# Loading and multiplying the first two blocks of k's weights among q's first blocks

## The chip, the core and the metric

The kernel runs on one core of a Trainium2 chip. The core has five engines with queues of their own: TensorE (PE; its weight loads, PEld, overlap its matmuls), VectorE (DVE), ScalarE (ACT), GpSimd (POOL) and SyncE (SP), which here issues nearly all transfers (DMA) from the chip's memory (HBM) to on-chip memory (SBUF). PE writes to accumulators in eight banks of PSUM. The metric is the device time of one execution in microseconds (us).

## The reference

The reference is one decoder layer over 256 tokens of width 1024. Its start, cut to what matters here:

```
h = rms_norm(x, attn_norm_g)                 # x * rsqrt(mean(x^2) + eps) * g
proj = h @ w_in                              # 1024 x (6 x 512 + 8 + 2048)
qa, ka, va, qb, kb, vb, f_logit, g_logit = split(proj)
qa = partial_rope(rms_norm(qa heads), pos)   # the same for ka
o_a = moba_attention(qa, ka, va)             # causal: 256 tokens are one block
o_b = forgetting_attention(rms_norm(qb), rms_norm(kb), vb, log_sigmoid(f_logit + b))
merged = gate_a * (o_a @ w_moba) + gate_b * (o_b @ w_fox)
x = x + merged @ w_out
x = x + conv_ffn(rms_norm(x))                # 1024 -> 2 x 2816 -> 1024
```

All is float32. The norm's factor per token, rsqrt(mean(x^2)), is a number per row of the product, so it can be applied after the product with w_in; g belongs to the rows of w_in and goes in before.

## The kernel before, in words

**Products of split numbers.** PE multiplies float32 operands in a shortened format (fp32r). To keep precision, each operand is split into a high part and a low part: ACT copies it into the high part (`whi` for weights, `xh` for x), DVE subtracts to get the low part (`wlo`, `xl`). A product is then three: xh·whi, xh·wlo, xl·whi.

**Blocks.** `project(m, pt, h)` forms one of six products of x with 512 columns (m = 0 is q, 1 is k, 2 is v of the first branch, 3 to 5 those of the second). The 1024 inputs are eight k-blocks of 128; h chooses four of them. For each k-block there are three pairs of matmuls of 512 columns (the two of a pair, t = 0 and 1, are the two halves of the tokens and write to two banks). Before the change q's eight blocks are multiplied first, then k's first four, then the matmul for the norm (`norm1`, L227), the products of the forget gate (L318), then k's other four, v's, and so on.

**The lead.** q's weights and x itself come in eight transfers `lead[k]`, each 384 KB: 256 values of x and 512 weights for each of 128 rows. `lead(p)` issues two of them and records the splitting of two blocks: `split_x(k)` makes `xh` and `xl` with the norm's weights g (for k = 0 the high part is made on DVE, L160, later on ACT, L162; the low part on DVE, L163), L102 makes `whi` on ACT, L103 `wlo` on DVE. g comes in a transfer of its own (4 KB), issued by ACT.

**The other weights.** `load` brings every further chunk of 1 MB into one of three buffers `raw` (SP issues; L131) and splits it in halves of 1024 columns (L134 on ACT, L135 on DVE) into one of six pairs of buffers `whi`/`wlo`. k's first chunk alone is fetched as two transfers of 512 KB. A raw buffer is free when both halves are split, a `whi`/`wlo` pair when PE has used it. At most eight transfers of SP stand open: each waits for the one eight before it.

**The norm.** Behind the split of k's first chunk ACT squares x (L181, two instructions), DVE adds the squares up (L183 to L186, with a `wlo` of L135 between), PE sums over partitions (L227), and DVE and ACT turn that into the factor `rs` (L202 to L207, with ACT's L203 and L204). DVE copies the forget gate's products (L320) between. Then `finish_qk` normalizes the heads of q and k and rotates them (up to L279), and `turn_qk` transposes them on PE (L295): first q's, sixteen loads and matmuls, then k's sixteen.

**The order.** On PE the instructions stand in the order in which the code issues them. On ACT, DVE and SP a scheduler sets the order when the program is built; on the chip each engine then works strictly in that order.

**The start.** DVE clears a tile of 512 bf16 numbers, with which PE does eight matmuls whose result nobody reads (L170, the warm-up); then the first block begins.

The table names the lines around the change, before and after (the same code under two numbers):

| step | before | after |
|---|---|---|
| transfers of the lead | L95 | L101, L102, L104 |
| transfers of k's first two blocks | in L131 | L107 |
| whi, wlo of the lead (ACT, DVE) | L102, L103 | L117, L120 |
| whi, wlo of k's first two blocks | in L134, L135 | L124, L125 |
| xh for k = 0 (DVE), xh (ACT), xl (DVE) | L160, L162, L163 | L184, L186, L190 |
| warm-up matmuls | L170 | L197 |
| whi, wlo of other weights | L134, L135 | L160, L161 |
| matmuls of `project` | L249 | L272 |

Of the kernel before, what the change touches and what calls it, by code (L numbers as in the profile page):

```python
# [8 lines left out]
F32 = mybir.dt.float32  # L9
# [8 lines left out]
P = 128  # L18
# [12 lines left out]
RB, HB, AHEAD = 3, 6, 5  # L31
NWARM = 8
GAPS = (160, 192)
# [8 lines left out]
def decoder_block(ctx, tc, a, out):  # L42
# [7 lines left out]
    def T(shape, tag, bufs=1, dt=F32):  # L50
        return sb.tile(shape, dt, tag=tag, bufs=bufs, name=tag)
# [21 lines left out]

    lt = T([P, KT, LW], "lead")
    xT = lt[:, :, 0:S]
# [16 lines left out]
    def lead(p):  # L92

        for k in (2 * p, 2 * p + 1):
            nc.sync.dma_start(lt[:, k], a["lead"][k])  # L95
        hi = T([P, 1024], "whi", HB, F32R)
        lo = T([P, 1024], "wlo", HB, F32R)
        for j in range(2):
            w = lt[:, 2 * p + j, S:]
            s = slice(j * W4, (j + 1) * W4)  # L100
            split_x(2 * p + j)  # L101
            whi = nc.scalar.activation(hi[:, s], w, AF.Copy)  # L102
            nc.vector.tensor_tensor(lo[:, s], w, hi[:, s].bitcast(F32), op=ALU.subtract)  # L103
        split[("qkv", 0, p // 2), p % 2] = (hi, lo, whi)  # L104

    def home(n):
# [9 lines left out]
    def load(upto):  # L116
        while state["next"] <= min(upto, 2 * len(chunks) - 1):  # L117
            i, h = divmod(state["next"], 2)
            state["next"] += 1
            if i < 2:  # L120
                lead(2 * i + h)
                continue
            c = chunks[i]
            if h == 0:  # L124
                w = 1024 if i == 2 else 2048  # L125
                src = a[c[0]]
                for j in (c[1] - (c[0] == "qkv"), *c[2:]):
                    src = src[j]
                raw = state["raw"] = T([P, 2048], "raw", RB)
                for j in range(2048 // w):  # L130
                    nc.sync.dma_start(raw[:, j * w:(j + 1) * w], src[:, j * w:(j + 1) * w])  # L131
            raw = state["raw"][:, h * 1024:(h + 1) * 1024]
# [14 lines left out]
    sm = T([P, C_END], "sm")  # L147
    g1 = T([P, KT], "g1")
    nc.scalar.dma_start(g1, a["g1"])

# [6 lines left out]
    def split_x(k):  # L157
        g, x = g1[:, k:k + 1], xT[:, k]
        if k == 0:
            nc.vector.tensor_scalar_mul(xh[:, k], x, g)  # L160
        else:  # L161
            nc.scalar.activation(xh[:, k], x, AF.Copy, scale=g)  # L162
        nc.vector.scalar_tensor_tensor(xl[:, k], x, g, xh[:, k].bitcast(F32), op0=ALU.mult, op1=ALU.subtract)  # L163


    warm = T([P, 512], "sq", 2, BF16)
    nc.vector.memset(warm, 0.0)
    wp = bank()
    for j in range(NWARM):
        nc.tensor.matmul(wp, warm[:, 0:P], warm, start=True, stop=True)  # L170

# [67 lines left out]
    V = T([P, NT, 2 * W4], "V")  # L239

    def project(m, pt, h):
        for hh in range(2):
            wh, wl = use(("qkv", m, h), hh)
            for k2 in range(2):
                k = 4 * h + 2 * hh + k2
                rh, rl = (pairs(w[:, k2 * 512:(k2 + 1) * 512]) for w in (wh, wl))
                for i, (lhs, rhs) in enumerate(((xh, rh), (xh, rl), (xl, rh))):
                    for t in range(NT):
                        nc.tensor.matmul(pt[t], lhs[:, k, t * P:(t + 1) * P], rhs, start=(k == 0 and i == 0), stop=(k == KT - 1 and i == 2))  # L249

# [489 lines left out]
def _layout(i):  # L740
# [9 lines left out]
    lead = np.concatenate([x.T.reshape(KT, P, S), w6[:, :W4].reshape(KT, P, W4)], 2)  # L750
    a["lead"] = c(lead)
    a["wf"] = c(k128(w[:, 6 * W4:6 * W4 + NH]))
# [11 lines left out]
    sm = np.empty((P, C_END), f)  # L764
    a["g1"] = c(i["attn_norm_g"][0].reshape(KT, P).T)
    sm[:, C_G2:C_G2 + 8] = i["ffn_norm_g"][0].reshape(KT, P).T
# [41 lines left out]
```

## Time and profile before

| | |
|---|---|
| time, median of 3 runs | 353.95 us (353.94 to 354.75) |
| the profiled execution | 353.87 us, of which the span of its instructions 352.1 us |
| PE busy | 346.8 us, 99% |
| DVE busy | 282.8 us, 80% |
| ACT busy | 225.2 us, 64% |
| from HBM | 67.65 MB, 195 GB/s over the span |

In the lines of the profile, L12 is line 12 of the kernel. A row of the timeline gives the start in us, the time to the end of the last of its instructions, the engine, line and operation, the tiles (written<-read), the shape, how many instructions were merged (x2), and in brackets how long the engine had idled before and what ended that. A row for a stretch gives its bounds and length in us, then the busy time of PE, PEld, DVE, ACT and POOL with the number of instructions in brackets, the clock recorded for PE as a share, the share in which the 16 transfer engines were busy, and GB/s. In the page's list of queues stand packets, megabytes and the share of the 16 engines' time. PE's matmuls overlap, so the start of one to the start of the next tells its pace, not its length.

### The profile page before, as it was taken

Reading aid. Unit: us, or ns where it says so; the run is one execution under the profiler, and the core shown is the slowest. Engines: PE = TensorE matmul, PEld = TensorE weight load, DVE = VectorE, ACT = ScalarE, POOL = GpSimd, SP = SyncE. Lnnn points to the kernel's source line nnn. Section 1 sums busy time; section 2 is a strip of 40 time slices with the busy share of each in tenths; the row PEclk is TensorE's granted clock in tenths of the full one; section 3 lists DMA queues with packets and bytes.
Section 4 is the critical chain, followed back from the end, with each engine's and each line's share of the span. In section 5 each row is a group of like instructions: output and inputs, shape, how many; then the busy total and the mean of one; then the engine's idle time right before and its main releaser. Section 6 shows DMA issues by size and latency. Waiting matters only on the chain.

```text
span 352.1 us, 5895 instructions
## 1 busy us (share of the span) xinstructions
PE 346.8 (99%) x2282; PEld 312.2 (89%) x2282; DVE 282.8 (80%) x533; ACT 225.2 (64%) x404; POOL 1.3 (0%) x8
## 2 busy tenths in 40 slices
PE   8999999999999999999999999999999999999995
PEld 4888888899989989998899989989898989989885
DVE  4899979995796568994489999897879788797633
ACT  5977575858698566662497975765665666565320
POOL 0000000000000000000000000000000000000000
PEclk9999999999999999999999999999999999999999
DMA  7988865566333607865119556674565456550003
GB/s 267 407 340 302 302 236 167 201 232 238 123 122 108 248 6 253 336 247 169 72 45 374 196 224 239 217 262 151 208 239 171 192 235 203 173 223 2 0 0 121
DMA packets 13597, 69.09 MB, mean 196 GB/s; under 512 B 1529, under 2 KB 4737, under 8 KB 6145
## 3 DMA queue, kind: packets, MB, share of 16 engines
q1 hardware_dynamic: 12368, 67.65, 52.8%
q10 hardware_dynamic: 1200, 1.06, 0.9%
q8 instruction: 18, 0.29, 0.3%
q14 instruction: 11, 0.08, 0.1%
HBM read 67.65 MB, written 1.06 MB: 195 GB/s over the span
## 4 chain that ended last, share of the span: by engine, by line
PE 97%; DMA 1%; ACT 0%; SPq 0%; DVE 0%; issue 0%
PE bank L654 22%; PE bank L249 17%; PE bank L700 16%; PE bank L655 11%; PE bank L581 6%; PE bank L454 4%; PE bank L455 4%; PE bank L456 4%; PE bank L551 2%; PE bank L553 2%; PE bank L552 2%; PE bank L387 2%; PE bank L428 2%; DMA lead<-in_lead 1%; PE bank L414 1%; PE bank L295 1%
## 5 line engine op out<-in xcount | busy, mean ns | idle before, releaser
L135 DVE TENSOR_TENSOR wlo<-raw,whi 128x1024 fp32r<-128x1024 f32 x91 | 110.6, 1223 | 24.1 <-ACT whi L134 23.6
L134 ACT ACTIVATE whi<-raw 128x1024 fp32r<-128x1024 f32 x91 | 94.9, 1053 | 39.1 <-PE bank L654 12.8
L654 PE MATMUL bank<-pp,whi 128*128 128x512 f32 x240 | 79.3, 382 | 0.0
L655 PE MATMUL bank<-pp,wlo 128*128 128x256 f32 x240 | 65.4, 273 | 0.0
L654 PEld LDWEIGHTS bank<-pp,whi 128*128 128x128 f32 x240 | 45.4, 189 | 6.3
L655 PEld LDWEIGHTS bank<-pp,wlo 128*128 128x128 f32 x240 | 46.1, 192 | 0.2
L454 PE MATMUL bank<-xh,whi 128*128 128x256 f32 x128 | 35.4, 277 | 0.0
L455 PE MATMUL bank<-xl,whi 128*128 128x256 f32 x128 | 35.2, 275 | 0.0
L456 PE MATMUL bank<-xh,wlo 128*128 128x256 f32 x128 | 35.2, 275 | 0.0
L249 PE MATMUL bank<-whi,xh 128*128 128x512 f32 x96 | 29.0, 384 | 0.3 <-DVE xh L160 0.2
L249 PE MATMUL bank<-wlo,xh 128*128 128x512 f32 x96 | 28.8, 382 | 0.0
L249 PE MATMUL bank<-whi,xl 128*128 128x512 f32 x96 | 28.6, 379 | 0.0
L454 PEld LDWEIGHTS bank<-xh,whi 128*128 128x128 f32 x128 | 24.6, 192 | 0.3 <-DVE nm L392 0.2
L455 PEld LDWEIGHTS bank<-xl,whi 128*128 128x128 f32 x128 | 24.6, 192 | 0.0
L456 PEld LDWEIGHTS bank<-xh,wlo 128*128 128x128 f32 x128 | 24.6, 192 | 0.0
L700 PE MATMUL bank<-whi,qT 128*128 128x512 f32 x72 | 22.4, 379 | 0.0
L670 DVE TENSOR_TENSOR sq<-bank,lows 128x256 f32<-128x256 f32 x44 | 18.2, 418 | 4.9 <-ACT lows L669 4.9
L249 PEld LDWEIGHTS bank<-whi,xh 128*128 128x128 f32 x96 | 17.7, 189 | 4.3 <-ACT whi L102 1.2
L249 PEld LDWEIGHTS bank<-wlo,xh 128*128 128x128 f32 x96 | 17.9, 189 | 3.4 <-DVE wlo L103 1.0
L669 ACT ACTIVATE lows<-bank 128x256 f32<-128x256 f32 x44 | 15.8, 367 | 7.5 <-PE bank L655 7.5
L249 PEld LDWEIGHTS bank<-whi,xl 128*128 128x128 f32 x96 | 18.1, 189 | 2.6
L654 PE MATMUL bank<-pp,bias 128*128 128x512 f32 x56 | 18.9, 385 | 0.0
(196 smaller groups left out, 704.6 us busy)
## 6 DMA issues: line engine op xcount, KB each, us to landing
raw<-in_wu SPq DMA_DIRECT2D x22, 1024.0 KB, 4.8
raw<-in_wd SPq DMA_DIRECT2D x11, 1024.0 KB, 4.8
raw<-in_qkv SPq DMA_DIRECT2D x9, 1024.0 KB, 7.1
raw<-in_wg SPq DMA_DIRECT2D x8, 1024.0 KB, 4.9
raw<-in_wb SPq DMA_DIRECT2D x4, 1024.0 KB, 4.8
raw<-in_wo SPq DMA_DIRECT2D x4, 1024.0 KB, 5.4
lead<-in_lead SPq DMA_DIRECT2D x8, 384.0 KB, 5.9
raw<-in_qkv SPq DMA_DIRECT2D x2, 512.0 KB, 7.7
```

What stands on the lines that cost most here:

```text
L134: whi = nc.scalar.activation(hi, raw, AF.Copy)
L135: wlo = nc.vector.tensor_tensor(lo, raw, hi.bitcast(F32), op=ALU.subtract)
L249: nc.tensor.matmul(pt[t], lhs[:, k, t * P:(t + 1) * P], rhs, start=(k == 0 and i == 0), stop=(k == KT - 1 and i == 2))
L454: nc.tensor.matmul(o, wh[:, w], rh, start=(k == 0 and i == 0), stop=False)
L455: nc.tensor.matmul(o, wh[:, w], rl, start=False, stop=False)
L456: nc.tensor.matmul(o, wl[:, w], rh, start=False, stop=(k == KT - 1 and i == 1))
L581: nc.tensor.matmul(acc[t][dh], lhs[:, k, t * P:(t + 1) * P], rhs, start=(k == 0 and i == 0), stop=(k == KT - 1 and i == 2))
L654: nc.tensor.matmul(two[i], wh[:, w], both, start=(k == 0), stop=False)
L655: nc.tensor.matmul(two[i][:, 0:S], wl[:, w], high, start=False, stop=(k == KT - 1))
L669: nc.scalar.activation(lows[:, i:i + 1].rearrange("p b (a t) -> p b a t", a=2), apart(two[i][:, S:2 * S], 1), AF.Copy)
L670: nc.vector.tensor_tensor(halves(ev[:, i:i + 1]), apart(two[i][:, 0:S], 1), halves(lows[:, i:i + 1]), op=ALU.add)
L700: nc.tensor.matmul(o, lhs, rhs, start=(first and i == 0), stop=(end and i == 2))
```

## The change

It does five things, all at the start of the program. (1) The first lead block comes as two transfers: its weights (256 KB), and then x with the norm's weights g in front (132 KB); g's own transfer is gone, and g1 is now the first eight columns of the tile `lead`. (2) The first two k-blocks of k's weights, which were the first 512 KB of k's first chunk, come as two transfers of 256 KB, one behind the first lead block and one behind the second, and are split there, into one more pair of `whi`/`wlo`; the chunk's second half is fetched later as before. (3) PE multiplies each of these two blocks right behind the q block with the same k, and k's loop leaves them out later. (4) For the first block the low part of the weights is made ahead of the low part of x. (5) There are seven warm-up matmuls instead of eight, on a tile of 128 numbers that is read four times over.

```diff
-NWARM = 8
+NWARM = 7
...
-    lt = T([P, KT, LW], "lead")
+    lead_all = T([P, KT + KT * LW], "lead")
+    g1 = lead_all[:, 0:KT]
+    lt = lead_all[:, KT:].rearrange("p (k w) -> p k w", k=KT)
...
     def lead(p):
+        if p == 0:
+            raw = state["raw"] = T([P, 2048], "raw", RB)
+            k_hi, k_lo = T([P, 1024], "whi", HB, F32R), T([P, 1024], "wlo", HB, F32R)
         for k in (2 * p, 2 * p + 1):
-            nc.sync.dma_start(lt[:, k], a["lead"][k])
+            if k == 0:
+                nc.sync.dma_start(lt[:, 0, S:], a["lead_w"])
+                nc.sync.dma_start(lead_all[:, 0:KT + S], a["lead_x"])
+            else:
+                nc.sync.dma_start(lt[:, k], a["lead"][k - 1])
+            if p == 0:
+                s = slice(k * W4, (k + 1) * W4)
+                nc.sync.dma_start(raw[:, s], a["qkv"][0][0][:, s])
         hi = T([P, 1024], "whi", HB, F32R)
         lo = T([P, 1024], "wlo", HB, F32R)
         for j in range(2):
-            w = lt[:, 2 * p + j, S:]
+            k = 2 * p + j
+            w = lt[:, k, S:]
             s = slice(j * W4, (j + 1) * W4)
-            split_x(2 * p + j)
+            if k:
+                split_x(k)
+                split_low(k)
             whi = nc.scalar.activation(hi[:, s], w, AF.Copy)
-            nc.vector.tensor_tensor(lo[:, s], w, hi[:, s].bitcast(F32), op=ALU.subtract)
+            if k == 0:
+                split_x(k)
+            wlo = nc.vector.tensor_tensor(lo[:, s], w, hi[:, s].bitcast(F32), op=ALU.subtract)
+            if k == 0:
+                after(split_low(k), wlo)
+            if p == 0:
+                k_whi = nc.scalar.activation(k_hi[:, s], raw[:, s], AF.Copy)
+                nc.vector.tensor_tensor(k_lo[:, s], raw[:, s], k_hi[:, s].bitcast(F32), op=ALU.subtract)
         split[("qkv", 0, p // 2), p % 2] = (hi, lo, whi)
+        if p == 0:
+            split[("qkv", 1, 0), 0] = (k_hi, k_lo, k_whi)
...
+            if (i, h) == (2, 0):
+                continue
             c = chunks[i]
-            if h == 0:
-                w = 1024 if i == 2 else 2048
+            if i == 2:
+                nc.sync.dma_start(state["raw"][:, 1024:], a["qkv"][0][0][:, 1024:])
+            elif h == 0:
...
-    warm = T([P, 512], "sq", 2, BF16)
+    warm = T([P, 128], "sq", 2, BF16)
...
-        nc.tensor.matmul(wp, warm[:, 0:P], warm, start=True, stop=True)
+        nc.tensor.matmul(wp, warm, warm[:, None, :].to_broadcast([P, 4, P]), start=True, stop=True)
...
+    def block(pt, w2, k):
+        rh, rl = (pairs(w[:, k % 2 * 512:(k % 2 + 1) * 512]) for w in w2)
+        for i, (lhs, rhs) in enumerate(((xh, rh), (xh, rl), (xl, rh))):
+            for t in range(NT):
+                nc.tensor.matmul(pt[t], lhs[:, k, t * P:(t + 1) * P], rhs, start=(k == 0 and i == 0), stop=(k == KT - 1 and i == 2))
+
     def project(m, pt, h):
         for hh in range(2):
...
+            if (m, h, hh) == (1, 0, 0):
+                continue
+            w2 = use(("qkv", m, h), hh)
+            if (m, h, hh) == (0, 0, 0):
+                wk = split.pop((("qkv", 1, 0), 0))[:2]
+            for k in (4 * h + 2 * hh, 4 * h + 2 * hh + 1):
+                block(pt, w2, k)
+                if m == 0 and k < 2:
+                    block(pk, wk, k)
```

What that does to SP's queue, at the start of the program (`lead` is the tile of x, q's weights and now g; `raw` holds k's weights), before:

```order
L95 DMA lead<-in_lead 128x768 x8
L173 DMA sm<-in_smalls 128x156
L131 DMA raw<-in_qkv 128x1024 x2
L131 DMA raw<-in_qkv 128x2048
L189 DMA cst<-in_consts 128x832
```

and now:

```order
L101 DMA lead<-in_lead_w 128x512
L102 DMA lead<-in_lead_x 128x264
L107 DMA raw<-in_qkv 128x512
L104 DMA lead<-in_lead 128x768
L107 DMA raw<-in_qkv 128x512
L104 DMA lead<-in_lead 128x768 x6
L200 DMA sm<-in_smalls 128x156
L151 DMA raw<-in_qkv 128x1024
L157 DMA raw<-in_qkv 128x2048
```

k's first 512 KB have moved from behind the eight lead blocks into the first five transfers; k's second 512 KB have the same bytes ahead of them as before, now with g's 4 KB among them.

On DVE, from the last lead block to the norm's factor (`bias` is here the buffer of the summed squares, `qn` that of the squares), before:

```order
L103 TENSOR_TENSOR wlo<-lead,whi 128x512
L135 TENSOR_TENSOR wlo<-raw,whi 128x1024 x2
L183 TENSOR_TENSOR bias<-qn 128x512
L184 TENSOR_TENSOR bias<-qn 128x512
L185 TENSOR_TENSOR bias<-bias 128x512
L135 TENSOR_TENSOR wlo<-raw,whi 128x1024
L186 TENSOR_TENSOR bias<-bias 128x256
L135 TENSOR_TENSOR wlo<-raw,whi 128x1024
L202 TENSOR_SCALAR rsv<-bank 128x2
```

and now:

```order
L120 TENSOR_TENSOR wlo<-lead,whi 128x512
L161 TENSOR_TENSOR wlo<-raw,whi 128x1024
L210 TENSOR_TENSOR bias<-qn 128x512
L211 TENSOR_TENSOR bias<-qn 128x512
L212 TENSOR_TENSOR bias<-bias 128x512
L161 TENSOR_TENSOR wlo<-raw,whi 128x1024
L213 TENSOR_TENSOR bias<-bias 128x256
L161 TENSOR_TENSOR wlo<-raw,whi 128x1024
L229 TENSOR_SCALAR rsv<-bank 128x2
```

One low part of 1024 columns is gone from here (it stands as two of 512 columns among the first lead blocks); the rest stands as it did, and from there on the order is unchanged.

On PE, from the first real matmul on (before, banks 189 and 190 are q's; after, 190 and 191 are q's, 192 and 193 k's; `whi_98` and `whi_101` are q's first weights, `whi_94` k's), before:

```order
L249 MATMUL bank_189<-whi_98,xh_83 128x512
L249 MATMUL bank_190<-whi_98,xh_83 128x512
L249 MATMUL bank_189<-wlo_99,xh_83 128x512
L249 MATMUL bank_190<-wlo_99,xh_83 128x512
L249 MATMUL bank_189<-whi_98,xl_84 128x512
L249 MATMUL bank_190<-whi_98,xl_84 128x512
L249 MATMUL bank_189<-whi_98,xh_83 128x512
L249 MATMUL bank_190<-whi_98,xh_83 128x512
```

and now:

```order
L272 MATMUL bank_190<-whi_101,xh_81 128x512
L272 MATMUL bank_191<-whi_101,xh_81 128x512
L272 MATMUL bank_190<-wlo_102,xh_81 128x512
L272 MATMUL bank_191<-wlo_102,xh_81 128x512
L272 MATMUL bank_190<-whi_101,xl_82 128x512
L272 MATMUL bank_191<-whi_101,xl_82 128x512
L272 MATMUL bank_192<-whi_94,xh_81 128x512
L272 MATMUL bank_193<-whi_94,xh_81 128x512
L272 MATMUL bank_192<-wlo_95,xh_81 128x512
L272 MATMUL bank_193<-wlo_95,xh_81 128x512
L272 MATMUL bank_192<-whi_94,xl_82 128x512
L272 MATMUL bank_193<-whi_94,xl_82 128x512
```

Behind q's first block now stand the six matmuls of k's first block, where q's second block followed; likewise behind q's second block.

More of the change, by code (lines that the diff above doesn't have):

```diff
@@ L129, in load @@
                 raw = state["raw"] = T([P, 2048], "raw", RB)
-                for j in range(2048 // w):
-                    nc.sync.dma_start(raw[:, j * w:(j + 1) * w], src[:, j * w:(j + 1) * w])
+                nc.sync.dma_start(raw, src)
             raw = state["raw"][:, h * 1024:(h + 1) * 1024]
@@ L147, in decoder_block @@
     sm = T([P, C_END], "sm")
-    g1 = T([P, KT], "g1")
-    nc.scalar.dma_start(g1, a["g1"])
     def col(c, n=1):
@@ L162, in split_x, with split_low @@
             nc.scalar.activation(xh[:, k], x, AF.Copy, scale=g)
-        nc.vector.scalar_tensor_tensor(xl[:, k], x, g, xh[:, k].bitcast(F32), op0=ALU.mult, op1=ALU.subtract)
-    warm = T([P, 512], "sq", 2, BF16)
+    def split_low(k):
+        g, x = g1[:, k:k + 1], xT[:, k]
+        return nc.vector.scalar_tensor_tensor(xl[:, k], x, g, xh[:, k].bitcast(F32), op0=ALU.mult, op1=ALU.subtract)
+    warm = T([P, 128], "sq", 2, BF16)
     nc.vector.memset(warm, 0.0)
@@ L239, in decoder_block @@
     V = T([P, NT, 2 * W4], "V")
+    def block(pt, w2, k):
[3 more added lines that the diff above has]
+                nc.tensor.matmul(pt[t], lhs[:, k, t * P:(t + 1) * P], rhs, start=(k == 0 and i == 0), stop=(k == KT - 1 and i == 2))
     def project(m, pt, h):
         for hh in range(2):
[L243 to L249, printed above, removed]
+            if (m, h, hh) == (1, 0, 0):
[7 more added lines that the diff above has]
+                    block(pk, wk, k)
     def finish_v(pt, m):
@@ L750, in _layout @@
     lead = np.concatenate([x.T.reshape(KT, P, S), w6[:, :W4].reshape(KT, P, W4)], 2)
-    a["lead"] = c(lead)
+    a["lead"] = c(lead[1:])
+    a["lead_w"] = c(lead[0, :, S:])
+    a["lead_x"] = c(np.concatenate([k128(i["attn_norm_g"][0][:, None])[:, :, 0], lead[0, :, :S]], 1))
     a["wf"] = c(k128(w[:, 6 * W4:6 * W4 + NH]))
@@ L764, in _layout @@
     sm = np.empty((P, C_END), f)
-    a["g1"] = c(i["attn_norm_g"][0].reshape(KT, P).T)
     sm[:, C_G2:C_G2 + 8] = i["ffn_norm_g"][0].reshape(KT, P).T
```

## The prediction, made before the result was known

> **What bounds the kernel now.** I read the page first, then the engines' timelines of the first 24 us, the transfers' rates in stretches, and last the two places where TensorE (PE) takes something just as it is made.
>
> ```profile
> span 352.1 us, 5895 instructions
> PE 346.8 (99%) x2282; PEld 312.2 (89%) x2282; DVE 282.8 (80%) x533; ACT 225.2 (64%) x404; POOL 1.3 (0%) x8
> ```
>
> PE idles for 5.3 us in all, so no reordering can bring more than that. What is idle or slow at the front shows in PE's timeline:
>
> ```profile
> 1.19 3.25 PE L170 MATMUL bank<-sq 128*128 128x512 bf16 x8 [1.19 <-DVE ones L175]
> 4.58 0.67 PE L249 MATMUL bank<-whi,xh 128*128 128x512 f32 x2 [0.15 <-DVE xh L160]
> 5.19 0.70 PE L249 MATMUL bank<-wlo,xh 128*128 128x512 f32 x2
> 5.73 0.59 PE L249 MATMUL bank<-whi,xl 128*128 128x512 f32 x2
> 6.16 0.59 PE L249 MATMUL bank<-whi,xh 128*128 128x512 f32 x2
> 9.12 0.59 PE L249 MATMUL bank<-whi,xl 128*128 128x512 f32 x2
> 20.78 0.59 PE L249 MATMUL bank<-whi,xl 128*128 128x512 f32 x2
> 21.21 0.50 PE L227 MATMUL bank<-ones,bias 128*128 128x1 f32 x4
> ```
>
> A block (one k of 128 rows) is three pairs of matmuls. From 9.12 to 21.21 there are 28 pairs without a stall: 0.432 us a pair, 1.296 a block. The eight pairs ahead of 9.12 would take 3.46 at that pace but last from 4.58, 4.54. So waits for data cost 1.08 us, and with them the twelve blocks ahead of the norm's matmul (L227) behave as if they began at 21.21 - 12 x 1.296 = 5.66. That 1.08, and the lateness of 4.58, are what the change can win.
>
> What is waited for:
>
> ```profile
> 0.86 0.27 DVE L167 MEMSET sq<- 128x256 uint32 x1 [0.86 <-PEq L801]
> 3.78 0.63 ACT L102 ACTIVATE whi<-lead 128x512 fp32r<-128x512 f32 x1 [1.77 <-DMA lead<-in_lead]
> 4.09 0.35 DVE L160 TENSOR_SCALAR xh<-lead,g 128x256 fp32r<-128x256 f32 x1 [2.95 <-DMA g<-in_g]
> 4.45 0.69 DVE L103 TENSOR_TENSOR wlo<-lead,whi 128x512 fp32r<-128x512 f32 x1
> 4.79 0.51 ACT L162 ACTIVATE xh<-lead,g 128x256 fp32r<-128x256 f32 x1 [0.38 <-DMA lead<-in_lead]
> 6.78 0.51 ACT L162 ACTIVATE xh<-lead,g 128x256 fp32r<-128x256 f32 x1 [0.96 <-DMA lead<-in_lead]
> ```
>
> The first block is here by 3.78, the norm's weights (g) only by 4.09, the second block by 4.79, the third not before 6.78. The transfers' rates say why (last column, GB/s):
>
> ```profile
> 2.50:4.25 1.75, 1.75 (x6) 0.55 (x4) 0.16 (x1) 0.47 (x1) 0.00 (x0) 1.00 0.99 369
> 4.25:6.00 1.75, 1.60 (x7) 0.98 (x7) 1.74 (x5) 1.19 (x3) 0.00 (x0) 1.00 0.89 256
> 6.00:10.00 4.00, 3.84 (x17) 2.55 (x16) 3.19 (x7) 3.22 (x7) 0.00 (x0) 1.00 1.01 398
> ```
>
> The transfer engines are busy throughout, yet from 4.25 to 6.00 they move 256 GB/s. Against 398 that loses 1.75 x 142/398 = 0.62 us. At 398 a lead block (384 KB, 0.99 us) comes faster than PE uses one (1.296), so PE starves only at the front.
>
> **The change, part by part.** *Start.* The weights, two thirds of the first block, come alone: whi can start up to a third of a block's 0.99 earlier (0.33), or not at all if the first bytes' delay rules. x and g land with the block's last bytes, about when the block landed before: between 3.78 and the old 4.09. Split x then takes 0.35, whi 0.63, and PE followed the later of them by 0.14 (4.44 to 4.58). So the first pair comes at 4.3 at best and, with whi still begun at 3.78, at 4.55; I take 4.35, since the weights are in front in the queue. The Trainium skill (DMA: Bandwidth & Descriptors, Rules for kernel authors) advises against two transfers in place of one, there for halves of the partitions: they share the same engines and serialize. By that rule the first pair comes at 4.55 and the sum below stays as it is, because 0.2 here is not on the path that ends last. No run here shows yet which holds. The shorter memset ends up to 0.2 before 1.13; seven warm-up matmuls at 3.25/8 = 0.41 are over by 4.06, before 4.35, so they delay nothing; the eighth could have.
>
> *First blocks.* VectorE (DVE) still makes xh, wlo, xl in turn; the pattern of the rows (pairs at +0, +0.61, +1.15, next block +1.58) gives 4.35 to 5.93. Then k's first block runs to 7.23. Its weights are 256 KB, 0.71 us at 369 GB/s behind x: landed at 4.5 to 4.8, high part 0.63 later, low part behind xl on DVE, 0.69, at 6.1; PE wants them at 5.93 and 6.36. No stall. ACT and DVE gain waits here (on those 256 KB); behind each is queued the second block's split, which needs a transfer issued later, so the wait adds nothing.
>
> q's second block ends 1028 KB into the queue. Before, 768 KB were here at 4.79 and 1152 at 6.78: by these ends I interpolate 6.1. Then 0.51 and 0.61 on ACT: 7.2, in time for 7.23; the low part 0.69 later holds the second pair by about 0.27. k's second block covers the third of q (landed at 8.1 by 398 GB/s, low part at 9.9). So q's third starts at 10.1, and eight further blocks bring PE to the norm's matmul at 10.1 + 8 x 1.296 = 20.5; without the slow stretch 4.35 + 0.28 + 12 x 1.296 = 20.2. Against 21.21 this alone would be 0.7 to 1.0 us. It covers k's later weights as well: they are multiplied in the old order.
>
> *What then ends last.* The matmul at 21.21 needs the sum of x squared, and that chain hangs on the transfer of k's second half, not on PE:
>
> ```profile
> 14.51 1.06 ACT L134 ACTIVATE whi<-raw 128x1024 fp32r<-128x1024 f32 x1 [0.20 <-DMA raw<-in_qkv]
> 15.48 2.00 ACT L181 ACTIVATE qn<-lead 128x1024 f32<-128x1024 f32 x2
> 17.50 0.69 DVE L184 TENSOR_TENSOR bias<-qn 128x512 f32<-128x512 f32 x1
> 18.84 1.32 DVE L135 TENSOR_TENSOR wlo<-raw,whi 128x1024 fp32r<-128x1024 f32 x1
> 20.08 0.41 DVE L186 TENSOR_TENSOR bias<-bias 128x256 f32<-128x256 f32 x1
> 20.42 1.21 DVE L135 TENSOR_TENSOR wlo<-raw,whi 128x1024 fp32r<-128x1024 f32 x1
> 21.64 1.07 PE L318 MATMUL bank<-lead,wf 128*32 128x256 f32 x16
> 21.75 0.16 DVE L202 TENSOR_SCALAR rsv<-bank 128x2 f32<-128x2 f32 x1
> 21.94 0.20 ACT L203 ACTIVATE rsv<-rsv 128x2 f32<-128x2 f32 x1 [2.58 <-DVE rsv L202]
> 22.29 1.99 ACT L134 ACTIVATE whi<-raw 128x1024 fp32r<-128x1024 f32 x2
> 22.86 0.42 DVE L320 COPY pT<-bank 128x256 f32<-128x256 f32 x1 [0.53 <-PE bank L318]
> 23.58 0.16 DVE L207 SCALAR_TENSOR_TENSOR rs<-rsv 128x2 f32<-128x2 f32 x1
> ```
>
> The same bytes go ahead of that transfer in one saturated queue, and the order from L183 on is unchanged; that the first half's conversion leaves ACT and DVE here frees nothing, as the second's stands behind its own landing at 14.51. So L186 still ends at 20.49 and PE can start the norm at 20.54: at most 0.67 earlier, wherever PE stands. DVE takes part of that back. L202 stands behind the conversion that ends at 21.63; consecutive DVE rows overlap by 0.08, so it moves from 21.75 to 21.54, 0.21, and ACT's conversion behind it from 22.29 to 22.08, its first half done at 23.14. The copy L320 follows PE (0.67 earlier, but behind DVE's work until 22.11) at 22.19, and L207 would start at 22.91. The next low part, until now right behind L207 at 23.66, then waits for ACT: 23.18. DVE is 0.48 earlier, not 0.67.
>
> That stays so until PE takes k's finished heads:
>
> ```profile
> 23.70:44.70 21.00, 21.00 (x113) 18.36 (x113) 20.85 (x41) 14.67 (x21) 0.00 (x0) 1.00 0.83 302
> 44.23 0.58 PEld L295 LDWEIGHTS bank<-cst,qn 64*128 64x128 f32 x16
> 44.40 0.28 DVE L279 TENSOR_TENSOR qn<-p,p 128x128 f32<-128x128 f32 x1
> ```
>
> DVE (fourth figure) works 20.85 of 21.00 us here: nothing waits in it, so a start 0.48 earlier passes through and no more. L279 ends k's rotation at 44.68; the sixteen loads of q's heads begin at 44.23 and k's follow at about 44.74. There is no slack. PE, 0.67 earlier, must wait for a DVE that is 0.48 earlier.
>
> *More packets.* Bounds from the queues' rows:
>
> ```profile
> q1 hardware_dynamic: 12368, 67.65, 52.8%
> q10 hardware_dynamic: 1200, 1.06, 0.9%
> ```
>
> Net there are 128 rows more (two parts of the first block, two of k's half, less g). On q10 a packet costs 0.009 x 352.1 x 16 / 1200 = 0.042 us; over 16 engines 128 of them are 0.34 us. The low end is 0, since the bytes are the same; pieces of 1 to 2 KB are nearer to q1's size than to q10's, so I take a tenth of the upper end, 0.03. It delays the transfer at 14.51 one for one.
>
> Sum: 0.48 - 0.03 = 0.45 us. The profiled execution (353.87 us, 1.8 around its span) becomes 353.42; the median shown is 0.08 above it, so **353.5 us**.
>
> **Rivals.** *PE's front rules (0.20).* If the slow stretch does not come back when the transfers' order and places differ, k's second half lands up to 0.62 earlier, the squares' chain no longer binds, and PE keeps 0.7 to 1.0: 353.1, at best 352.9. For it: nothing in the rows ties the stretch to a place. Against it: it may as well come twice.
>
> *Hidden (0.12).* Packets at 0.34, or the landing that much later for another reason: 0.48 - 0.34 = 0.14, that is 353.8. Then PE waits longer at the norm and at k's heads for just what it won.
>
> *Slower through the queue (0.12).* Three sources are touched in the first microseconds instead of one. Should two more stretches like the one at 4.25 arise ahead of k's second half, it lands 1.24 later: 0.48 - 1.24 = -0.76, 354.7; with one, -0.14, 354.1. It decides from a landing after 14.99. I set 354.2.
>
> *Slower through PE's clock (0.08).* The warm-up matmuls take 0.41 each, real ones 0.216, so PE starts at about half speed; by 5.73 pairs are 0.43 apart, so it is at full speed. There is one warm-up less, and an idle gap behind it. If half speed lasted twice the warm-up's 3.25, to 7.5, 3.8 pairs from 4.35 on would lose 0.39 each, 1.5; the waits in them hide 0.55, and PE reaches the norm at 20.5 + 0.95 = 21.45: 0.24 later than before, 354.2. It decides from half speed beyond 7.0. The Trainium skill (TensorE: Matmul & The Clock Gate, Part 1) gives a reason for it: the full clock is granted after a window of about 3.4 us of activity that runs freely, so its phase differs from run to run. In this trace half speed ends between 1.19 and 5.73, which agrees; that it varies no row shows.
>
> That the change doesn't do what it says is excluded by the order of the instructions: k's products of blocks 0 and 1 stand behind q's.
>
> **How the numbers follow.** Forecast 0.48, front rules 0.20, hidden 0.12, queue 0.12, clock 0.08. The range runs from 352.9, the front's best, to 354.3, the two slower cases; the forecast's own is 353.3 to 353.8. What this kernel can tell from no change is 0.3%, 1.06 us: below 352.89 or above 355.01. Faster takes the outer part of the front's case and what I may have missed, 0.10; slower the second stretch or a late clock, 0.04; the same 0.86.
>
> **What would show it.** First L272 pair near 4.35; k's pairs without a gap; PE idle ahead of the norm's matmul (20.2 to 20.5, until 20.54) and, new, ahead of the sixteen loads of k's heads near 44.3. ACT's conversion of k's second half still near 14.5. It is wrong if that starts before 14 or after 15, if PE does not wait at either place, or if the pairs behind the first stay 0.6 and more apart.

## The result, and the profile after

The changed kernel takes 356.14 us (median of 6 runs, 355.34 to 356.55); the kernel before took 353.94 beside it (6 runs, 353.33 to 354.75). The ratio is 1.0056, 95% interval 1.0038 to 1.0075: 2.2 us slower, where 353.5 was forecast and the range ended at 354.3.

The page of the profiled execution (356.05 us) and PE's timeline at its start:

```profile
span 354.2 us, 5896 instructions
PE 347.7 (98%) x2281; PEld 313.6 (89%) x2281; DVE 282.9 (80%) x534; ACT 225.4 (64%) x405; POOL 1.3 (0%) x8
...
0.99 3.17 PE L197 MATMUL bank<-sq 128*128 128x512 bf16 x7 [0.99 <-DVE ones L202]
5.44 1.19 PE L272 MATMUL bank<-whi,xh 128*128 128x512 f32 x2 [1.28 <-DVE xh L184]
6.43 1.06 PE L272 MATMUL bank<-wlo,xh 128*128 128x512 f32 x2
7.28 1.06 PE L272 MATMUL bank<-whi,xl 128*128 128x512 f32 x2
8.13 1.05 PE L272 MATMUL bank<-whi,xh 128*128 128x512 f32 x2
8.99 0.63 PE L272 MATMUL bank<-wlo,xh 128*128 128x512 f32 x2
9.45 0.59 PE L272 MATMUL bank<-whi,xl 128*128 128x512 f32 x2
9.88 0.59 PE L272 MATMUL bank<-whi,xh 128*128 128x512 f32 x2
...
22.83 0.50 PE L254 MATMUL bank<-ones,bias 128*128 128x1 f32 x4
```

PE stands idle for 1.28 us ahead of the first pair, which comes at 5.44 (4.58 before); the pairs are 0.85 us apart until 8.99, half speed (0.43 later on); and the norm's matmul comes at 22.83, 1.62 later than before. Who is late shows on DVE and ACT, in the first rows behind their waits:

```profile
4.94 0.35 DVE L184 TENSOR_SCALAR xh<-lead 128x256 fp32r<-128x256 f32 x1 [4.00 <-DMA lead<-in_lead_x]
...
6.72 0.63 ACT L124 ACTIVATE whi<-raw 128x512 fp32r<-128x512 f32 x1 [2.84 <-DMA raw<-in_qkv]
7.92 0.51 ACT L186 ACTIVATE xh<-lead 128x256 fp32r<-128x256 f32 x1 [0.57 <-DMA lead<-in_lead]
...
16.20 1.06 ACT L160 ACTIVATE whi<-raw 128x1024 fp32r<-128x1024 f32 x1 [0.50 <-DMA raw<-in_qkv]
```

x comes at 4.94, k's first block at 6.72, the second lead block at 7.92 (4.79 before), k's second half at 16.20 (14.51 before). All wait for transfers. The last sum of the squares ends at 22.17, 0.66 ahead of the norm's matmul, so here PE's own late blocks bind, and not that chain:

```profile
21.76 0.41 DVE L213 TENSOR_TENSOR bias<-bias 128x256 f32<-128x256 f32 x1
```

The rates by stretch (last column GB/s, the one ahead of it the busy share of the 16 transfer engines), three rows of the changed kernel and then, for the kernel before, 2.5 to 6.0 us:

```profile
2.50:4.25 1.75, 1.66 (x4) 0.30 (x2) 0.00 (x0) 0.63 (x1) 0.00 (x0) 1.00 0.79 155
4.25:6.00 1.75, 0.56 (x1) 0.50 (x2) 1.06 (x3) 0.00 (x0) 0.00 (x0) 1.00 0.86 166
6.00:10.00 4.00, 4.00 (x13) 3.23 (x12) 2.48 (x5) 2.37 (x5) 0.00 (x0) 1.00 1.02 392
...
2.50:6.00 3.50, 3.35 (x12) 1.53 (x11) 1.91 (x5) 1.66 (x3) 0.00 (x0) 1.00 0.94 313
```

In the same three stretches it was 369, 256 and 398 before. The transfers crawl at 160 GB/s from 2.5 to 6.0 us (313 before) and are as fast as before from then on. At 398 that loses 3.5 x (313 - 160)/398 = 1.35 of the 1.69 us by which k's second half is late.

A second loss stands far behind, where ACT waits for a block of `wb` and PE for what follows from it. ACT's wait before was 1.98, and PE had none:

```profile
127.65 1.07 ACT L160 ACTIVATE bias<-raw 128x1024 fp32r<-128x1024 f32 x1 [2.87 <-DMA raw<-in_wb]
130.64 0.58 PE L449 MATMUL bank<-cst,s 64*128 64x64 f32 x11 [0.84 <-DVE lead L496]
```

PE is 1.6 late up to here and 2.49 behind it; the landing of the last output gives 0.4 back, and the span is 2.1 longer.

### The profile page after: what moved, and what is told of

It reads as the page before. It is cut to its first block, busy times and chain, and to the rows that moved or that the text cites. A ratio compares the mean times of both kernels' runs of the same rounds, so it can differ in the third digit from the quotient of the medians.

```text
span 354.2 us, 5896 instructions
## 1 busy us (share of the span) xinstructions
PE 347.7 (98%) x2281; PEld 313.6 (89%) x2281; DVE 282.9 (80%) x534; ACT 225.4 (64%) x405; POOL 1.3 (0%) x8
## 4 chain that ended last, share of the span: by engine, by line
PE 95%; DMA 3%; DVE 1%; ACT 0%; issue 0%; SPq 0%; ACTq 0%
PE bank L689 22%; PE bank L272 18%; PE bank L735 16%; PE bank L690 11%; PE bank L616 6%; PE bank L489 3%; PE bank L490 3%; PE bank L491 3%; PE bank L586 2%; DMA raw<-in_wb 2%; PE bank L587 2%; PE bank L588 2%; PE bank L422 2%; PE bank L463 2%; DMA lead<-in_lead_x 1%; PE bank L449 1%
## 5 line engine op out<-in xcount | busy, mean ns | idle before, releaser
L161 DVE TENSOR_TENSOR wlo<-raw,whi 128x1024 fp32r<-128x1024 f32 x90 | 109.3, 1222 | 23.2 <-ACT whi L160 22.9
L160 ACT ACTIVATE whi<-raw 128x1024 fp32r<-128x1024 f32 x90 | 93.8, 1053 | 38.2 <-PE bank L689 12.5
L272 PE MATMUL bank<-whi,xh 128*128 128x512 f32 x96 | 29.9, 394 | 1.3 <-DVE xh L184 1.3
```

What stands on the lines that cost most here:

```text
L160: whi = nc.scalar.activation(hi, raw, AF.Copy)
L161: wlo = nc.vector.tensor_tensor(lo, raw, hi.bitcast(F32), op=ALU.subtract)
```

## The experiments

The measure in all of them is the rate between 2.5 and 6.0 us, the start of ACT's conversion of k's second half, and the time beside that of the kernel before in the same session (353.94 to 354.26). The sessions ran on different chips.

**The changed kernel again.**

> The changed kernel once more, to see what of its first trace repeats. Theory 'places' (the transfers crawl because the first microseconds touch several arrays and rows that lie apart): the crawl is there again, 3.25 to 5.75 us far below 200 GB/s, the second half of k's weights is converted at 16 to 17 us (16.20 the first time), time 355.5 to 356.5. Theory 'chance' (the first trace had a bad start): that conversion lies anywhere between 14.5 and 16. The wait of 2.9 us for a block of in_wb near 127 us: if it is the change's own, it comes again and the end is 2.4 us later than before; if it is chance, it may be gone and the end is 1.6 later.

355.83 us, ratio 1.0052 (1.0035 to 1.0070). The second trace:

```profile
2.50:6.00 3.50, 3.30 (x10) 1.25 (x8) 1.43 (x3) 0.63 (x1) 0.00 (x0) 1.00 0.75 186
...
4.36 0.69 PE L272 MATMUL bank<-whi,xh 128*128 128x512 f32 x2 [0.20 <-DVE xh L184]
4.95 0.70 PE L272 MATMUL bank<-wlo,xh 128*128 128x512 f32 x2
5.48 0.60 PE L272 MATMUL bank<-whi,xl 128*128 128x512 f32 x2
7.96 0.70 PE L272 MATMUL bank<-whi,xh 128*128 128x512 f32 x2 [1.88 <-ACT whi L124]
...
16.78 1.06 ACT L160 ACTIVATE whi<-raw 128x1024 fp32r<-128x1024 f32 x1 [0.50 <-DMA raw<-in_qkv]
```

The crawl repeats (186 GB/s, 16.78). The late x and the half speed do not: the first pair is at 4.36 and the next 0.59 behind it. They are not the cause; now PE waits 1.88 for k's first block, and the norm's matmul is as late as in the first trace (22.95).

**More warm-up.** `NWARM = 7` becomes 11.

> The change with eleven warm-up matmuls instead of seven, so that PE has no idle gap between 4.16 and 5.44 us. If PE's late full speed (pairs 0.86 us apart until 9.0 in the profile after, where data for the second block stood ready at 9.0) carries part of the loss: full speed by 5.5, the second block of q starts at 9.0 instead of 9.88 and then waits a little for its low part, norm's matmul 0.5 to 0.9 earlier, time 355.2 to 355.6. If the speed is granted late whatever PE does, or the transfers alone set the pace: 355.9 to 356.4.

355.64 us, 1.0038 (1.0013 to 1.0063); 156 GB/s, k's second half at 17.11. PE is busy until its data come (first pair at 5.30, pairs 0.43 apart from 5.97 on), and the loss stays: the clock is at most a few tenths of it.

**The parts alone.** First, the split: the kernel before with the first block as two transfers and g beside x (k untouched, eight warm-up matmuls). Second, the interleaving: the change without the split, g in a transfer of its own, eight warm-up matmuls.

```diff
 # first kernel, against before (lt is laid out as in the change)
-nc.sync.dma_start(lt[:, k], a["lead"][k])
+if k == 0:
+    nc.sync.dma_start(lt[:, 0, S:], a["lead_w"])
+    nc.sync.dma_start(lead_all[:, 0:KT + S], a["lead_x"])
+else:
+    nc.sync.dma_start(lt[:, k], a["lead"][k - 1])
```

```diff
 # second kernel, against the change
-            if k == 0:
-                nc.sync.dma_start(lt[:, 0, S:], a["lead_w"])
-                nc.sync.dma_start(lead_all[:, 0:KT + S], a["lead_x"])
-            else:
-                nc.sync.dma_start(lt[:, k], a["lead"][k - 1])
+            nc.sync.dma_start(lt[:, k], a["lead"][k])
```

> The kernel before with one part of the change: the first block as two transfers, weights in front, the norm's weights beside x; k's weights, products and the eight warm-up matmuls as before. Theory A (k's early transfers, a third array with rows of 2 KB that lie 8 KB apart, stop the transfer engines; packets of 700 to 900 ns stand at 3.45 to 3.63 us in the profile after): no crawl beyond the old one, the first pair at 4.2 to 4.5 instead of 5.44, time 353.4 to 354.0. Theory B (the engines crawl in a fixed stretch of time, about 3 to 5.5 us, whatever is fetched): the crawl is there as before the change, 256 GB/s in 4.25 to 6.00, time 353.7 to 354.3. Theory C (the split itself, with its small rows of 1056 bytes, is at fault): x lands after 4.5 us, first pair after 5, time over 354.8.

> The change without its first part: the first block whole, the norm's weights in a transfer of their own, eight warm-up matmuls; k's first two blocks loaded and multiplied between q's as in the change. Theory A: the crawl from 3.2 to 5.7 us is there at full strength (under 200 GB/s), because k's transfers stand behind the first block; the first pair comes at 4.6 as before, since the first block is ahead of it, but the second block of q and all behind it are late, norm's matmul at 22.0 or later, time 355.2 to 356.5. Theory B: crawl as before the change, norm's matmul at 20.5 to 21.2, time 353.4 to 354.2. Theory C: as B.

Split alone: 354.71, 1.0010 (0.9989 to 1.0031), 288 GB/s, k's second half at 15.34. Interleaving alone: 355.28, 1.0024 (1.0005 to 1.0043), 233 GB/s, 15.66. Both make the transfers slower, by 0.83 and 1.15 us at that half; the sum is about what the change loses (1.69 and 2.27). The first of the two kernels fits none of its three theories whole: slower than A and B have it, but with its first pair at 4.22, against C. It also has g in front; g in front alone, below, costs as much time on this base (354.73), with k's second half at 14.94. So on the kernel before no run shows a price of the split in time.

**Where the bytes lie.** Two kernels: k's two early blocks from a small array of their own without gaps; and all early transfers from one array `front`, in which they lie in the order in which they are fetched.

```diff
-nc.sync.dma_start(raw[:, s], a["qkv"][0][0][:, s])
+nc.sync.dma_start(raw[:, s], a["kfirst"][k])       # first kernel
...
-nc.sync.dma_start(lt[:, k], a["lead"][k - 1])
-nc.sync.dma_start(raw[:, s], a["qkv"][0][0][:, s])
+nc.sync.dma_start(lt[:, k], front(LW))             # second kernel: front(w) is
+nc.sync.dma_start(raw[:, s], front(W4))            # the next 128 x w of the array
```

> The change with one size altered: k's first two blocks come from an array of their own in which each block's 256 KB lie together (rows of 2 KB without gaps), all else as in the change. If the 8 KB stride of the rows is what chokes the engines (theory A, first form): over 300 GB/s from 3.2 to 5.7 us, first pair near 4.4, time 353.4 to 354.2. If it is the touching of one more array (theory A, second form): crawl as in the change, 355.3 to 356.5. Theory B: as the change, 355.3 to 356.5.

> The change with the same transfers in the same order, but all from one array in which they lie one behind the other, as the lead did before: weights of block 0, g and x of block 0, k's first block, the second lead block, k's second block, and so on. Theory 'places': nothing is touched out of order, the rates of the first 6 us are at least those of before (369, then 256 GB/s), first pair at 4.2 to 4.5, k's second half converted at 14.4 to 15.0, time 353.3 to 354.0. Theory 'number of transfers' (each further transfer at the start costs, wherever it reads): that conversion at 15.4 to 16.2 as with k's early blocks in an array of their own (15.58) and the time 354.5 to 355.5.

```profile
2.50:6.00 3.50, 3.27 (x10) 1.23 (x8) 1.43 (x3) 1.24 (x2) 0.00 (x0) 1.00 0.90 271
...
15.58 1.06 ACT L160 ACTIVATE whi<-raw 128x1024 fp32r<-128x1024 f32 x1 [0.49 <-DMA raw<-in_qkv]
21.61 0.61 PE L254 MATMUL bank<-ones,bias 128*128 128x1 f32 x4 [0.28 <-DVE bias L213]
```

These rows are the first's. 354.84, 1.0007 (0.9986 to 1.0029), for the first; 354.47, 1.0014 (0.9998 to 1.0029), 279 GB/s, 15.60 for the second. Rows without gaps take away more than half of the loss. One array instead of three adds nothing to that, so it is not the number of sources.

**A whole first block.** From the one array, with g, x and weights of block 0 in one transfer and eight warm-up matmuls; the same kernel twice. Then the split kernel of the last paragraph with eight warm-up matmuls, so that only the split differs. Then the whole first block with a split second one.

```diff
-nc.sync.dma_start(lt[:, 0, S:], front(W4))
-nc.sync.dma_start(lead_all[:, 0:KT + S], front(KT + S))
+nc.sync.dma_start(lead_all[:, 0:KT + LW], front(KT + LW))   # whole first block
...
-nc.sync.dma_start(lt[:, k], front(LW))                       # the split second block, k == 1
+nc.sync.dma_start(lt[:, 1, S:], front(W4))
+nc.sync.dma_start(lt[:, 1, 0:S], front(S))
```

> As the kernel with one array, but the first block is one transfer again, with g in front of x and of the weights, and eight warm-up matmuls. Theory 'places': rates as before, first pair at 4.3 to 4.6, k's second half converted at 14.4 to 15.0, the time 353.3 to 354.0, within 0.2 of the kernel with the split block. Theory 'number of transfers': with one transfer fewer it is 0.2 to 0.7 faster than the kernel with the split block, since splitting alone cost 0.70 us at the third block.

> The kernel with one array and whole blocks once more, for a narrower interval and a second trace. If its 0.14% are real, the ratio is again 0.997 to 0.9995 and k's second half is converted at 14.4 to 14.9; if they were chance, the ratio lies at 1.000 to 1.002. The wait near 128 us, which cost 0.9 us in its first trace and nothing in that of before, should come and go by chance: here anything from 0 to 1.

> The kernel with one array and a split first block (354.47 us), with eight warm-up matmuls instead of seven. It differs from the kernel with one array and a whole first block (353.84 and 353.54) by the split alone. If the split is what costs (the transfers of the first 6 us), k's second half is converted at 15.3 to 15.8 again and the time is 354.2 to 354.7. If the missing warm-up matmul was it (PE's clock), that conversion does not matter and the time falls to 353.5 to 353.9.

> The kernel with one array and a whole first block, but now the second lead block comes as two transfers, weights (256 KB) and then x (128 KB), from the same place in the array. What is told apart is why two transfers for the first block cost 1.0 us at k's second half (converted at 15.60 against 14.57). Theory 'any further transfer': an additional issue early in the queue costs the same wherever it stands: that conversion at 15.3 to 15.8, the time 0.4 to 0.7 over the kernel with whole blocks. Theory 'the first one' (only a short transfer with which the queue begins costs): 14.4 to 14.9 and no difference in time.

The rows of the whole first block (first trace), of the split one with eight warm-up matmuls, and of the split second one:

```profile
2.50:6.00 3.50, 3.27 (x10) 1.34 (x9) 1.78 (x4) 1.26 (x2) 0.00 (x0) 1.00 1.00 314
...
14.57 1.06 ACT L164 ACTIVATE whi<-raw 128x1024 fp32r<-128x1024 f32 x1 [0.75 <-DMA raw<-in_qkv]
...
2.50:6.00 3.50, 3.50 (x9) 1.85 (x8) 1.42 (x3) 1.21 (x2) 0.00 (x0) 1.00 0.93 284
...
15.84 1.06 ACT L165 ACTIVATE whi<-raw 128x1024 fp32r<-128x1024 f32 x1 [0.88 <-DMA raw<-in_qkv]
...
2.50:6.00 3.50, 3.50 (x9) 1.66 (x8) 1.89 (x4) 1.68 (x3) 0.00 (x0) 1.00 0.99 341
```

Whole: 353.84, 0.9986 (0.9970 to 1.0002), and 353.54, 0.9979 (0.9965 to 0.9992); 314 and 308 GB/s, k's second half at 14.57 and 15.15. Split, eight warm-up matmuls: 354.69, 1.0016 (1.0001 to 1.0031), 284 GB/s, 15.84. So the split costs 0.6 to 1.1 us and the eighth warm-up matmul is not it. A split second block, of nearly the same two widths, costs nothing: 353.37, 0.9986 (0.9973 to 0.9998), 341 GB/s, 14.36. So it is not one transfer more that costs, but a split of the first block; by what mechanism, no run shows. The interleaved kernels with a whole first block and no gaps are 0.4 to 0.7 us faster than the kernel before, by intervals of which two leave out 1 and one does not.

**The distance of the rows.** With a whole first block, k's early blocks are read as in the change (rows of 2 KB, 8 KB apart, in the array of all of k's first weights), then from an array of their own with 8, 9 (twice) and 4 KB; last, the change itself with 9 KB.

```diff
-nc.sync.dma_start(raw[:, s], front(W4))
+nc.sync.dma_start(raw[:, s], a["kpad"][:, s])     # a["kpad"]: 128 x 2304 (9 KB), 2048, 1024
```

> The change with only its first block undone to one transfer (g, x and weights in one row of 3104 bytes, eight warm-up matmuls); k's first two blocks are read as in the change, rows of 2 KB that lie 8 KB apart. Measured so far with whole first blocks: rows one behind the other 353.84 and 353.54 us (k's second half converted at 14.57 and 15.15), rows 9 KB apart 354.15 (14.85). Theory 'distance of 8 KB': clearly worse than 9 KB, that conversion at 15.4 to 16, the time 354.8 to 355.4. Theory 'any gap': as with 9 KB, 14.7 to 15.2 and 354.0 to 354.4; then the 1.1 us of the kernel that only interleaves came from g's own transfer.

> The kernel with a whole first block and k's first two blocks from an array of their own, now with rows 8 KB apart instead of 9 (354.15 us, 312 GB/s between 2.5 and 6.0 us). It tells the distance from the array: with 8 KB inside the array of all of k's weights it was 355.27 us and 210 GB/s. Theory 'distance of 8 KB': again 200 to 240 GB/s and 354.9 to 355.6 us. Theory 'array' (it is slow because other transfers read the same array): as with 9 KB, 300 to 320 GB/s and 353.9 to 354.4 us.

> The same kernel with whole blocks, but k's first two blocks are read from an array of their own whose rows of 2 KB lie 9 KB apart (in the change: 8 KB apart, in the kernel with one array: one behind the other). Theory 'distance of 8 KB' (rows at a power of two get in each other's way): with 9 KB k's second half is converted at 14.4 to 14.9, the time equals that of the kernel with one array. Theory 'any gap' (rows that lie apart are slow at the start of the queue): 15.4 to 16.0, as in the kernel that only interleaves (15.66), and the time 0.7 to 1.2 over that of the kernel with one array.

> The 9 KB once more beside the two others, on the same chip: 300 GB/s and more between 2.5 and 6.0 us and 353.8 to 354.4 us, if the first measurement holds.

> The same with rows 4 KB apart (the two blocks side by side in one array). Theory 'distance of 8 KB' says nothing of 4 KB by itself; if any power of two is bad, the rate lies between that of 8 KB (210) and that of rows without a gap (308 to 314), at 220 to 280 GB/s, and the time at 354.5 to 355.2; if it is 8 KB and more that is bad, 300 GB/s and more and 353.6 to 354.3.

> The change whole, with k's first two blocks from an array of their own whose rows lie 9 KB apart instead of 8. Theory 'distance of 8 KB': the loss of the rows that lie apart goes away, and what remains is that of the split first block: as with k's blocks in an array without gaps, conversion of k's second half at 15.4 to 15.8, time 354.5 to 354.9. Theory 'any gap': most of the loss stays, conversion at 15.9 to 16.8, time 355.2 to 356.0.

The row of 2.5 to 6.0 us, each from a kernel of its own: the change's array at 8 KB,

```profile
2.50:6.00 3.50, 3.43 (x11) 1.38 (x9) 1.44 (x3) 0.63 (x1) 0.00 (x0) 1.00 0.86 210
...
22.54 0.61 PE L258 MATMUL bank<-ones,bias 128*128 128x1 f32 x4 [0.28 <-DVE bias L217]
```

an array of its own at 8 KB,

```profile
2.50:6.00 3.50, 3.50 (x9) 1.74 (x8) 1.44 (x3) 0.63 (x1) 0.00 (x0) 1.00 0.90 234
```

and at 9 KB:

```profile
2.50:6.00 3.50, 3.47 (x11) 1.50 (x10) 1.97 (x4) 1.27 (x2) 0.00 (x0) 1.00 1.00 312
```

| rows of k's early blocks | first block whole | first block split |
|---|---|---|
| no gap | 314, 308 GB/s; 353.84, 353.54 us; late by -0.05, 0.06 us | 271, 279, 284; 354.84, 354.47, 354.69; 0.49, 0.51, 0.77 |
| 9 KB apart | 312, 309; 354.15, 354.33; -0.25, 0.19 | 284; 355.03; 0.47 |
| 4 KB apart | 286; 354.94; 0.97 | |
| 8 KB apart, own array | 234; 355.46; 1.04 | |
| 8 KB apart, as in the change | 210; 355.27; 1.43 (with g apart: 233; 355.28; 0.85) | 160, 186; 356.14, 355.83; 1.62, 1.73 (the change) |

"Late by" is how much later than before PE does, in the trace, the matmul that it did at 60 us (counted back from its last one). It leaves out all that differs between runs further behind.

The intervals: 8 KB 1.0031 (1.0019 to 1.0044) and, in an array of its own, 1.0036 (1.0022 to 1.0051); 9 KB 1.0004 (0.9993 to 1.0015) and 1.0003 (0.9992 to 1.0014); 4 KB 1.0011 (0.9996 to 1.0026); 9 KB and split 1.0022 (1.0009 to 1.0034). The distance decides, not the array: 1 KB more between the rows brings 1.1 us (355.46 against 354.33 in one session). 4 KB lies between in rate and time, but converts k's second half as late as 8 KB (16.06 against 15.90 and 16.51). With a whole first block the packets say the same; with a split one they scatter. Of the 128 packets of k's first block (2 KB each), a tenth takes longer than

```
8 KB:   370, 263, 449 (the change, the last with eleven warm-up matmuls)
        386 (whole)   373 (whole, own array)   365 (interleaving alone)
4 KB:   229 (whole)
9 KB:    84,  98 (whole)        206 (split)
no gap:  94,  99, 145 (whole)   84, 161, 400 (split)
```

ns, worked out from the transfer records; the shortest take 81 to 84.

The distance does not cost at all times. k's second block has the same rows at the same distance, and is read from 5.6 to 6.6 us on. With 8 KB a tenth of its packets takes longer than 115 to 244 ns (six traces), against 99 and 202 without a gap (whole); for the first block it was 263 to 449 against 94 and 99. k's second half, in rows of 4 KB that also lie 8 KB apart, has every packet at 159 ns in both traces of the change. So what 8 KB costs, it costs at the start of the program; why there, no run shows.

No gap is 0.5 us better than 9 KB in time, but not in rate, nor in PE's lateness at 60 us (-0.05 and 0.06 against -0.25 and 0.19). So these 0.5 us do not arise at the start, and where they arise is open.

**g in front alone.** The kernel before with g in front of its first lead block and without g's own transfer.

```diff
-nc.sync.dma_start(lt[:, k], a["lead"][k])
+nc.sync.dma_start(lead_all[:, 0:KT + LW], ...)     # k == 0: rows of 3104 bytes, g in front
...
-nc.scalar.dma_start(g1, a["g1"])
```

> The kernel before with one thing changed: g comes in front of the first lead block in its one transfer, and g's own transfer is gone. k is not touched. Theory 'the interleaving brings the gain of the kernel with one array': this kernel gains less than that one; first pair 4.3 to 4.6, the third block waits for its transfer as before (6.4 to 6.8), the time 353.9 to 354.3. Theory 'g in front is all of it': as fast as the kernel with one array and whole blocks (353.84 against 354.26 for before).

354.73, 1.0024 (1.0009 to 1.0040), slower than both theories have it. The kernel that also interleaves took 353.54 in the same session, 1.2 us less. That the interleaving (with the smaller edits (4) and (5)) brings these 1.2 us is not shown: at 60 us PE is 0.02 later than before in this kernel's trace and 0.06 in that one's. Why g in front costs 0.6 is open as well: the profiled execution (353.87) is among its fastest and does not show it.

**A transfer ahead.** The kernel before with 384 KB more in front of the first block, into a buffer that nobody reads.

```diff
+nc.sync.dma_start(T([P, 2048], "raw", RB)[:, 0:LW], a["lead"][0])
-nc.sync.dma_start(lt[:, k], a["lead"][k])
+nc.sync.dma_start(lt[:, k], a["lead"][k + 1])
```

> The kernel before with one more transfer in front: 384 KB, a copy of the first lead block, go to a buffer that nobody reads before the real blocks follow from the same array. Theory 'time' (the transfers are slow in the stretch from about 4.25 to 6.0 us whatever is fetched): the rate is below 300 GB/s between 4.25 and 6.0 and the third real block lands at 6.9 to 7.3, its second at 6.2 or later. Theory 'places' (the slow stretch belongs to what is read there, bytes 650 KB to 1.1 MB of the queue): the same stretch stands at those bytes of the array, so again 4.25 to 6.0, but it now hits the second block, or it goes with the third block and stands at 5.3 to 7.0. The time is about 1 us over before either way.

```profile
4.25:5.00 0.75, 0.53 (x2) 0.00 (x0) 0.03 (x1) 0.03 (x1) 0.00 (x0) 1.00 1.06 426
5.00:6.00 1.00, 0.35 (x2) 0.30 (x2) 0.96 (x3) 0.60 (x1) 0.00 (x0) 1.00 1.05 301
```

353.98 us (one run); the third real block's `xh` starts at 7.40. The first pair is 1.07 later, the last matmul only 0.42. So the slow stretch of the kernel before is not bound to 4.25 to 6.0 us. It came later and milder; with one trace of each, how much of that is chance is open.

## Why the prediction was wrong

The step that failed is a pair of sentences: k's first block "landed at 4.5 to 4.8", at 369 GB/s, and "the same bytes go ahead of that transfer in one saturated queue", with 0.34 us as the most that packets could cost. k's first block was converted at 6.72 and 7.27, and k's second half at 16.20 and 16.78 instead of near 14.5. I counted bytes and rows and left out how far the rows lie apart. The rate was taken from rows of 3 KB that lie one behind the other. The bound on packets was taken from queue q10, where g's small packets and 1032 packets of 1 KB run, these at 58 to 67 us; and the reason for using only a tenth of it was a misreading, since q10's mean packet is 0.88 KB and q1's 5.5, so that pieces of 1 to 2 KB are nearer to q10's. No row of before read 2 KB pieces 8 KB apart at the start (its 4 KB pieces 8 KB apart, at 10.7 to 13.9 us, went with a rate of 400 GB/s), and I should have said that this has no bound there. Two properties carry the loss: 8 KB between k's rows (1.1 us against 9 KB) and the split of the first block (0.6 to 1.1). Added to -0.5 for the version without either, and 0.5 for 9 KB against no gap, that is 1.7 to 2.2; measured, 1.6 and 2.2. PE's lateness at 60 us says the same without the two halves that cancel: 0.85 to 1.43 with 8 KB alone, 0.47 to 0.77 with the split alone, 1.62 and 1.73 with both.

The Trainium skill (DMA: Bandwidth & Descriptors, Latency and other measured facts) warns of rows a large power of two apart and advises a few KB of padding. It gives figures from 512 KB up; here, in the first 6 us, 8 KB is enough (210 and 234 GB/s against 312 and 309), and 1 KB of padding helps. By the rule of the same page of the Trainium skill (Rules for kernel authors), that two transfers to halves of the partitions serialize, the prediction had the first pair come at 4.55; in six of the eight traces with a split first block it came at 4.20 to 4.42. So the split cost nothing where the prediction looked, and its price stands further behind, at k's second half.

*First pair, 4.35.* 4.36 in one trace, 5.44 in the other. The first transfer did come early (`whi` started at 3.25 against 3.78 in the first trace), but x in rows of 1 KB landed as late as 4.94.

*q's second and third block, the norm at 20.2 to 20.5.* All late by the transfers: the second lead block came at 7.92 instead of 6.1, the norm's matmul at 22.83. In both traces of the change PE comes to the norm behind the end of the squares' chain (22.17 and 22.75), so these blocks bind there, where the prediction had PE wait for the chain.

*The squares' chain.* Where this chain binds, its size held, to 0.01 us. PE's start at the norm should be the landing's delay less 0.67. In the eight kernels whose traces have PE wait there, or start at the chain's end:

| k's second half later by | less 0.67 | norm's matmul later by |
|---|---|---|
| 0.34 (9 KB, first trace) | -0.33 | -0.34 |
| 0.64 (whole, no gap, second trace) | -0.03 | -0.03 |
| 1.07 (own array, no gap) | 0.40 | 0.40 |
| 1.09 (one array, split) | 0.42 | 0.42 |
| 1.33 (the same, eight warm-up) | 0.66 | 0.66 |
| 1.55 (4 KB) | 0.88 | 0.88 |
| 2.00 (8 KB, whole) | 1.33 | 1.33 |
| 2.60 (eleven warm-up) | 1.93 | 1.93 |

The row of the 4 KB kernel, with PE's wait:

```profile
22.09 0.60 PE L258 MATMUL bank<-ones,bias 128*128 128x1 f32 x4 [0.77 <-DVE bias L217]
```

*DVE gives part back at k's heads.* In the first trace of the version with a whole first block and no gap, PE reaches the norm 0.33 earlier than before (20.88) and k's heads 0.09 earlier. No slack, as forecast. The measured gain of that version, 0.42 and 0.54, has the size of the 0.45 in my sum, but that is chance: at 60 us PE is 0.05 earlier than before in one trace and 0.06 later in the other, so the gain does not come from these steps.

*The rivals.* "Slower through the queue" named the place and the point (a landing after 14.99), but sized it at 1.24 us from two more stretches like the known one; it was 1.69 and 2.27. By the prediction's own sum that gives 355.2 and 355.7; 356.14 and 355.83 were measured, with the wait for `wb` and PE's late blocks on top. "Through PE's clock" was seen: half speed until 8.99 in the first trace, beyond its 7.0. But the second trace and the kernel with eleven warm-up matmuls lose as much without it, since PE waits for transfers there anyway. That the two traces of one kernel differ agrees with the free-running window of the Trainium skill (TensorE: Matmul & The Clock Gate, Part 1); but only the first has PE idle for 1.28 us ahead of its first pair, and no run separates the two.

## What to carry to other kernels

When a change moves part of an array ahead, look at the address pattern of the moved piece: with rows of 2 KB, 8 KB apart, the first transfers went at two thirds to three quarters of the rate that they had without gaps, and repacking them in the order of their use, with a whole first block, turned a loss of 2 us into a gain of 0.5, of which the traces show only that the loss is gone. In this kernel it paid to leave the first transfer large: splitting it cost more than the early start was worth, while splitting the next cost nothing. A price for a transfer holds only for transfers of the same row length, distance and place in the queue; where none is in the trace, the bound is open upwards.

## What the hardware showed that was not expected

The rate of the first microseconds does not fall evenly with the distance of the rows: 308 to 314 GB/s with 9 KB or no gap, 286 with 4 KB, 210 to 234 with 8 KB, all with a whole first block. That rows at a power of two share something in the memory would fit; no run here shows what.

The wait for a block of `wb` near 127 us comes and goes in one and the same kernel. Two traces of the version with a whole first block:

```profile
126.11 1.07 ACT L164 ACTIVATE bias<-raw 128x1024 fp32r<-128x1024 f32 x1 [2.98 <-DMA raw<-in_wb]
129.10 0.58 PE L453 MATMUL bank<-cst,s 64*128 64x64 f32 x11 [0.94 <-DVE lead L500]
```

```profile
124.90 1.06 ACT L164 ACTIVATE bias<-raw 128x1024 fp32r<-128x1024 f32 x1 [1.67 <-DMA raw<-in_wb]
126.85 1.71 PE L453 MATMUL bank<-cst,s 64*128 64x64 f32 x48
```

PE loses 0.94 us in the first and nothing in the second. In the changed kernel it loses 0.84 and 0.42, and nothing in the trace with eleven warm-up matmuls; over all twenty traces PE waits there in eleven. So I count it to the spread of about 1.5 us between runs of one kernel. That the change makes the wait no more likely is not shown by two traces.
